# A network of two blocks with routed experts: the last expert's overflow block in one branch, and a hint for the branch on further blocks

## The chip, the cores and the metric

One core of one Trainium2 chip. The metric is the device time of one execution, in microseconds; the kernel before takes 1542.91 us (median of 3 runs, 1542.90 to 1544.29).

## What is computed

The input is 256 tokens of width 1024, all in float32. The first block has two layers. Each is a mixer (gated linear attention in layer 0, a gated linear recurrent unit, LRU, in layer 1), followed by a mixture of experts; shift, scale and gate of each come from a vector `c` through `ada_w`. The second block (weights `w_in`, `w_mod` and others) has three mixers side by side and a convolutional feed-forward part. What the change touches is the mixture of experts:

```python
scores = sigmoid(t @ router_w)
sel = scores + router_bias                     # 16 experts in 4 groups
grp = argmax over groups of the sum of the 2 largest sel in the group
expert_idx = the 2 largest sel inside grp      # 2 experts for each token
w = scores at expert_idx, divided by their sum
for e in range(16):
    he = silu(t @ w_gate[e]) * (t @ w_up[e])   # 1024 -> 512
    out = out + combine[:, e:e + 1] * (he @ w_down[e])   # 512 -> 1024
```

An expert's `combine` is zero for tokens that aren't routed to it, so only the routed tokens have to be worked on.

## The kernel before, in words

**An expert's tokens.** A rank says where a token stands among an expert's tokens. The first 64 tokens of an expert go through its main path: they are gathered by matmuls with one-hot matrices (`gather`, four experts at a time), go through `gate_up` (L904; SiLU and product L907 and L908), are transposed (`transp`, L913 and L915), go through `down` (L943; ACT L951 and DVE L954 scale the result into `y`), and `scatter` (L960) adds them with a one-hot matrix to `acc`, which stays in PSUM for a whole layer. `slots_of` (transposes L921, comparisons L923 and L924) makes the one-hot matrices `sa` for the scatter and `osa` for an overflow block.

**Overflow.** Where an expert has more than 64 tokens, the others go through blocks of 32. `vals[e]` is the number of such blocks, loaded into registers. A block has three parts: `block_x` (gather L988, weights L992, transposes L1001, scale and shift L1004 and L1005), `block_up` (L1013, transpose L1019, copy L1020) and `block_down` (L1027, scaling L1029 and L1030, scatter L1034). `blocks(e)` is an inner branch (L1045) with a loop in it, for the second block and more. With these inputs, experts 6 and 15 overflow in layer 0 and expert 12 in layer 1, each by one block, so the inner branch never enters its body.

**Where the branches stand.** Experts 0, 1 and 15 are *split*: a branch `up` behind gate and up (L1079) holds the inner branch, `block_x` and `block_up`, and a branch `ex` (L1100) at the expert's end holds `block_down`. The other experts have one branch, `ex`, with the whole block and then the inner branch. All five engines run each branch. `tc.mark_branch_hint_location` puts an instruction on each of the five engines that announces a branch, by its label, ahead of time, as one that is likely to jump (here: past the body). The outer branches have such a hint, ahead of the gate and up of their expert; the inner one has none.

**Weights.** `Stream` hands out weights from SBUF buffers of up to 2 MB, in one fixed order for the whole kernel: SP issues a transfer (L177 for gate and up, L179 for the others) as soon as a buffer is freed in the program and its readers are done. An expert holds three buffers: two halves of gate and up (read by L904 and L1013), and one of down (read by L943 and L1027). A split expert frees two of them behind its `up` branch and the third behind `ex`; the others free all three behind `ex`. Behind the last expert of layer 0 come the weights of the LRU layer (`ada_w`, first read by L442, and `lru_w_in`), behind that of layer 1 those of the second block: `w_in`, which ACT (L630) and DVE (L632) cut into pieces for the matmuls L641 to L643. The constants of the second block (`par_pk` among them) are loaded by L288, also on SP.

**The order of work** inside a stretch without branches is set by a list scheduler when the program is built; it moves half of the next expert's gate and up ahead of an expert's `ex` branch. The scatter of expert e is placed behind the gate and up of expert e + 1; the last expert's stands behind its `ex` branch, and behind that DVE adds `acc` to the state (L1112).

Of the kernel before, what the change touches and what calls it, by code (L numbers as in the profile page):

```python
# [20 lines left out]
NE = 16  # L21
# [212 lines left out]
class Net:  # L234
# [64 lines left out]
    def jobs(self):  # L299
# [32 lines left out]
        for n, j in self.late[0]:  # L332
            mod(n, j)
        self.marks["moe0"] = len(J)
        moe(0)
        self.marks["lru"] = len(J)
        w = A["lru_w_in"][0]
# [517 lines left out]
    def moe(self, l, m, late, aside={}):  # L855
        nc, tc = self.nc, self.tc
        shift, gate = m[:, 24:32], m[:, 40:48]
        with ExitStack() as st:
# [14 lines left out]
            vals = [nc.values_load(nblk[0:1, e:e + 1], min_val=0, max_val=6,  # L873
                                   skip_runtime_bounds_check_because="at most 256 tokens") for e in range(NE)]
# [98 lines left out]
            def tokens_of(oo, rk):  # L973

                for tt in range(2):
                    nc.vector.tensor_scalar(oo[:, tt], self.c("slots")[:, None, 0:32].to_broadcast([P, 4, 32]),
                                            rk[:, tt:tt + 1], None, op0=OP.is_equal)

            def block_x(e, oo):


                o = lambda tt: oo[:, tt].rearrange("p a b -> p (a b)")
                pg = [ps.tile([P, 512], F32, name="ps") for _ in range(2)]
                n = 0
                for tt in range(2):
                    for h in (hh, hl):
                        for c in range(2):
                            nc.tensor.matmul(pg[c], o(tt), h[:, tt, 512 * c:512 * c + 512], start=(n == 0), stop=(n == 3))  # L988
                        n += 1
                pw = ps.tile([P, 512], F32, name="ps")  # L990
                for tt in range(2):
                    nc.tensor.matmul(pw[:, :2], o(tt), whl[:, tt, e, :], start=(tt == 0), stop=(tt == 1))  # L992
                for g in range(4):
                    src = pg[g // 2][q(g), 256 * (g % 2):256 * (g % 2) + 256]
                    if g % 2:
                        nc.vector.tensor_copy(xt[q(g)], src)
                    else:
                        nc.scalar.activation(xt[q(g)], src, AF.Copy)
                pt = ps.tile([P, 512], F32, name="ps")
                for b in range(2):  # L1000
                    nc.tensor.transpose(pt[:, b * P:b * P + P], xt[:, b * P:b * P + P], self.ident)  # L1001
                quarters = lambda a: a.rearrange("p (b g s) -> p b g s", b=2, g=4)
                per_ft = lambda a: a.rearrange("p (g b) -> p b g", g=4)[:, :, :, None].to_broadcast([P, 2, 4, 32])
                nc.vector.tensor_tensor(quarters(xg), quarters(pt[:, :256]), per_ft(gs), op=OP.mult)  # L1004
                nc.vector.tensor_tensor(quarters(xg), quarters(xg), per_ft(shift), op=OP.add)  # L1005
                nc.vector.tensor_reduce(ow, pw[:, :2], axis=AX.X, op=OP.add)
# [35 lines left out]

            def blocks(e):

                with tc.If(vals[e] > 1):  # L1045
                    nc.vector.tensor_copy(rk, rank64[:, e, :])
                    nc.vector.tensor_copy(sc, sc64)
                    with tc.For_i(1, vals[e], 1):
                        nc.vector.tensor_scalar(rk, rk, 32.0, None, op0=OP.subtract)
                        nc.vector.tensor_scalar(sc, sc, 32.0, None, op0=OP.add)  # L1050
                        tokens_of(oo1, rk)
                        pt = ps.tile([P, 512], F32, name="ps")
                        for tt in range(2):
                            nc.tensor.transpose(pt[:, tt * P:tt * P + P], rank[:, tt, e:e + 1].to_broadcast([P, P]),
                                                self.ident)
                        nc.vector.tensor_scalar(osa1, pt[:, :T], sc, None, op0=OP.is_equal)
                        block_x(e, oo1)
                        block_up(e)
                        block_down(e, osa1)
# [8 lines left out]
            for e in range(NE):  # L1068
                g, j = e // 4, e % 4
                more = aside.get(e)  # L1070
                if more:
                    more(ps, sb)
                W[e] = [self.ws.take("moe") for _ in range(3)]
                split, end = e in (0, 1, NE - 1), e == NE - 1
                tc.mark_branch_hint_location(f"up{l}_{e}" if split else f"ex{l}_{e}", "LikelyTaken", engines=[mybir.EngineType.PE, mybir.EngineType.SP, mybir.EngineType.DVE, mybir.EngineType.Activation, mybir.EngineType.Pool])
                tokens_of(oo, rank64[:, e, :])
                he, last = gate_up(lambda k: XG[g][:, k, j, :], W[e])
                if split:
                    with tc.If(vals[e] > 0, label=f"up{l}_{e}"):  # L1079
                        blocks(e)  # L1080
                        block_x(e, oo)
                        block_up(e, "pgu")
                    self.ws.free(3 if more else 2)
                pt = ps.tile([P, 512], F32, name="ps")
                if split:
                    tc.mark_branch_hint_location(f"ex{l}_{e}", "LikelyTaken", engines=[mybir.EngineType.PE, mybir.EngineType.SP, mybir.EngineType.DVE, mybir.EngineType.Activation, mybir.EngineType.Pool])
                heT = transp(he, pt)
                if e:
                    with tc.issue_after(last):
                        scatter(*Y.pop(e - 1))  # L1090
                y = down(heT, W[e][2], WS[g][:, j:j + 1])
                with tc.issue_after(last):
                    Y[e] = y, slots_of(e, pt)
                    if g + 1 < 4 and j == 0:
                        onehot(g + 1)
                    if g + 1 < 4 and j == 3:
                        for i in range(4):
                            gather(g + 1, i)
                        slot_w(g + 1)
                with tc.If(vals[e] > 0, label=f"ex{l}_{e}"):  # L1100
                    if not split:
                        block_x(e, oo)
                        block_up(e)
                    block_down(e, osa, "pgu" if split else "py")
                    if not split:
                        blocks(e)
                if end:
                    scatter(*Y.pop(e))
                del W[e]
                self.ws.free(1 if split else 4 if more else 3)  # L1110
# [1072 lines left out]
```

## Time and profile before

| | |
|---|---|
| median of 3 runs | 1542.91 us |
| the profiled execution | 1545.11 us, its span 1543.3 us |
| TensorE's granted clock over the span | 0.975 of full speed |
| PE busy (matmuls) | 1436.0 us, 93% of the span |
| DVE, ACT, POOL busy | 808.2, 659.9, 76.0 us |
| DMA over the span | 406.25 MB, 263 GB/s on average |
| layer 0: mixer, then experts | to about 207 us, to 500 us |
| layer 1: mixer (LRU), then experts | to 645 us, to 921 us |
| second block | 921 us to the end |

How to read it: the span is the time from the first to the last instruction in the profile, and the profiled execution's own time is 1.8 us longer. An engine's busy time counts matmuls, vector and scalar work; branches and DMA issues belong to an engine's sequencer, shown with a q (PEq, SPq). In a timeline each row has a start, a duration and the work, and in brackets how long the engine stood idle before it and what ended that ("issue" where nothing the profile shows was waited for). Neighbouring instructions of one group are merged into one row.

### The profile page before, as it was taken

The numbers are of one execution on the slowest core, as the hardware profiler recorded it, in microseconds if no ns is written. First come the engines' busy times: TensorE is split into PE (matmuls) and PEld (weight loads), VectorE is DVE, ScalarE is ACT, GpSimd is POOL, SyncE is SP. The second block draws the span as 40 slices with busy tenths as digits, with TensorE's granted clock in tenths as the row PEclk, the third lists the DMA queues.
The fourth block names the chain that finished last, engine by engine and source line by source line (L and its number), as shares of the span: only waits on it lengthen the run. The fifth ranks groups of instructions, "written<-read, shape, count | busy, mean of one in ns | idle before, by whom it ended". The sixth has DMA issues, their size and how long they took to land. (4 is left out here: it accounts for less than half of the span.)

```text
span 1543.3 us, 24106 instructions
## 1 busy us (share of the span) xinstructions
PE 1436.0 (93%) x9234; PEld 995.1 (64%) x9234; DVE 808.2 (52%) x1930; ACT 659.9 (43%) x1347; POOL 76.0 (5%) x80
## 2 busy tenths in 40 slices
PE   5999978989897979889998889999999999999998
PEld 2565833434333658634434338898887889899998
DVE  3444531222222785422223237968876887876775
ACT  4534441212211565512123126666664565565553
POOL 0000110000000052200010000000000101100000
PEclk9999989999997999999999999999999999999999
DMA  9998586989999786786999864636634724995400
GB/s 362 386 386 297 207 336 255 342 316 360 393 392 379 280 315 239 297 325 237 395 394 391 306 222 141 218 114 215 220 137 136 254 74 165 318 362 195 137 1 28
DMA packets 193145, 406.25 MB, mean 263 GB/s; under 512 B 4514, under 2 KB 30754, under 8 KB 192691
## 3 DMA queue, kind: packets, MB, share of 16 engines
q1 hardware_dynamic: 192192, 402.75, 72.2%
q8 instruction: 121, 1.98, 0.5%
q10 hardware_dynamic: 754, 0.88, 0.2%
q14 instruction: 78, 0.63, 0.1%
HBM read 402.57 MB, written 1.05 MB: 262 GB/s over the span
## 5 line engine op out<-in xcount | busy, mean ns | idle before, releaser
L632 DVE TENSOR_TENSOR piece<-wt,piece 128x512 fp32r<-128x512 f32 (+1 forms) x364 | 276.2, 763 | 160.5 <-ACT piece L630 159.4
L630 ACT ACTIVATE piece<-wt 128x512 fp32r<-128x512 f32 (+1 forms) x368 | 248.4, 680 | 209.1 <-PE pd L643 154.3
L904 PE MATMUL pgu<-wt,xg 128*64 128x512 f32 x1024 | 252.5, 616 | 11.4 <-PEq L1100 6.2
L642 PE MATMUL pd<-hT,piece 128*128 128x256 f32 x624 | 177.6, 285 | 0.0
L641 PE MATMUL pd<-hT,piece 128*128 128x256 f32 x624 | 177.5, 285 | 0.0
L643 PE MATMUL pd<-hT,piece 128*128 128x256 f32 x624 | 176.8, 285 | 0.0
L904 PEld LDWEIGHTS pgu<-wt,xg 128*64 128x64 f32 x1024 | 74.8, 140 | 136.0 <-issue 130.0
L943 PE MATMUL py<-wt,heT 128*64 128x512 f32 x512 | 128.4, 616 | 3.8 <-ACT heT L915 3.8
L641 PEld LDWEIGHTS pd<-hT,piece 128*128 128x128 f32 x624 | 118.5, 190 | 4.8 <-ACT piece L630 2.2
L923 DVE TENSOR_SCALAR sa<-ps,par_cst 128x256 fp32r<-128x256 f32 x32 | 15.5, 484 | 201.6 <-issue 137.4
L642 PEld LDWEIGHTS pd<-hT,piece 128*128 128x128 f32 x624 | 118.6, 190 | 2.2 <-issue 2.0
L643 PEld LDWEIGHTS pd<-hT,piece 128*128 128x128 f32 x624 | 118.3, 190 | 2.1 <-issue 2.0
L951 ACT ACTIVATE y<-py,wsl 64x512 fp32r<-64x512 f32 x64 | 43.7, 683 | 174.0 <-PE py L943 157.7
L442 PE MATMUL pd<-wt,cond 128*32 128x512 f32 x576 | 86.5, 610 | 0.7 <-DMA wt<-ada_w 0.7
L943 PEld LDWEIGHTS py<-wt,heT 128*64 128x64 f32 x512 | 38.7, 141 | 70.7 <-issue 63.9
L907 ACT ACTIVATE he<-pgu 128x256 f32<-128x256 f32 x32 | 12.3, 384 | 145.2 <-PE pgu L904 135.9
L641 PE MATMUL pd<-s,piece 128*128 128x256 f32 x224 | 64.5, 289 | 3.5 <-ACT s L1274 2.3
L642 PE MATMUL pd<-piece,hT 128*128 128x512 f32 x160 | 66.1, 414 | 0.4 <-DVE piece L632 0.4
L643 PE MATMUL pd<-s,piece 128*128 128x256 f32 x224 | 63.4, 285 | 2.3 <-DVE piece L632 2.3
L643 PE MATMUL pd<-piece,hT 128*128 128x512 f32 x160 | 63.2, 398 | 0.0
L642 PE MATMUL pd<-s,piece 128*128 128x256 f32 x224 | 63.1, 283 | 0.0
L641 PE MATMUL pd<-piece,hT 128*128 128x512 f32 x160 | 57.9, 411 | 3.6 <-ACT piece L630 3.6
(595 smaller groups left out, 2879.0 us busy)
## 6 DMA issues: line engine op xcount, KB each, us to landing
wt<-moe_w_gate SPq DMA_DIRECT2D x64, 1024.0 KB, 11.2
wt<-moe_w_up SPq DMA_DIRECT2D x64, 1024.0 KB, 13.5
wt<-moe_w_down SPq DMA_DIRECT2D x32, 2048.0 KB, 15.6
wt<-ada_w SPq DMA_DIRECT2D x24, 2048.0 KB, 19.7
wt<-w_in SPq DMA_DIRECT2D x21, 2048.0 KB, 8.8
wt<-w_mod SPq DMA_DIRECT2D x12, 2048.0 KB, 8.5
wt<-w_up SPq DMA_DIRECT2D x22, 1024.0 KB, 12.3
wt<-gla_w_in SPq DMA_DIRECT2D x6, 2048.0 KB, 19.7
```

The lines of the kernel that those rows point to most:

```text
L442: nc.tensor.matmul(acc[32 * c:32 * c + 32, :], self.cond[:, k, :], w[:, k, :], start=(k2 == 0), stop=(k2 == 1))
L630: self.cast = nc.scalar.activation(hi, v, AF.Copy).ins
L632: (nc.gpsimd if low_on_pool else nc.vector).tensor_tensor(lo, v, hi.bitcast(F32), op=OP.subtract)
L641: mm(out, l[0], r[0], start=start, stop=False, **k)
L642: mm(out, l[0], r[1], start=False, stop=False, **k)
L643: mm(out, l[1], r[0], start=False, stop=stop, **k)
L904: last = nc.tensor.matmul(pgu[64 * hf:64 * hf + 64], xg(k), w[k // 4][:, :, k % 4, 256 * hf:256 * hf + 256], start=(k == 0), stop=(k == KT ...
L907: nc.scalar.activation(he, pgu[:, 0, :], AF.Silu)
L923: nc.vector.tensor_scalar(sa, pt[:, :T], self.c("slotcol"), None, op0=OP.is_equal)
L943: nc.tensor.matmul(py[64 * c:64 * c + 64, :], heT[:, b, 64 * hf:64 * hf + 64], wd[:, 2 * hf + b, 512 * c:512 * c + 512], start=(n == 0), s ...
L951: nc.scalar.activation(y[0:64, c], py[h], AF.Copy, scale=wsl[h])
```

## The change

Expert 15 is no longer split, in both layers. The inner branch gets a label, and those experts that aren't split run a hint for it where their `ex` branch has been entered, so only where the expert overflows.

```diff
--- before.py
+++ after.py
@@ -1042,7 +1042,7 @@
 
             def blocks(e):
 
-                with tc.If(vals[e] > 1):
+                with tc.If(vals[e] > 1, label=f"in{l}_{e}"):
                     nc.vector.tensor_copy(rk, rank64[:, e, :])
                     nc.vector.tensor_copy(sc, sc64)
                     with tc.For_i(1, vals[e], 1):
@@ -1071,7 +1071,7 @@
                 if more:
                     more(ps, sb)
                 W[e] = [self.ws.take("moe") for _ in range(3)]
-                split, end = e in (0, 1, NE - 1), e == NE - 1
+                split, end = e in (0, 1), e == NE - 1
                 tc.mark_branch_hint_location(f"up{l}_{e}" if split else f"ex{l}_{e}", "LikelyTaken", engines=[mybir.EngineType.PE, mybir.EngineType.SP, mybir.EngineType.DVE, mybir.EngineType.Activation, mybir.EngineType.Pool])
                 tokens_of(oo, rank64[:, e, :])
                 he, last = gate_up(lambda k: XG[g][:, k, j, :], W[e])
@@ -1099,6 +1099,7 @@
                         slot_w(g + 1)
                 with tc.If(vals[e] > 0, label=f"ex{l}_{e}"):
                     if not split:
+                        tc.mark_branch_hint_location(f"in{l}_{e}", "LikelyTaken", engines=[mybir.EngineType.PE, mybir.EngineType.SP, mybir.EngineType.DVE, mybir.EngineType.Activation, mybir.EngineType.Pool])
                         block_x(e, oo)
                         block_up(e)
                     block_down(e, osa, "pgu" if split else "py")
```

## Rows read from the trace of the kernel before

**Rows 1.** Windows: stretch, length, busy PE, PEld, DVE, ACT, POOL, PEclk, DMA share, GB/s.

```profile
207.00:500.00 293.00, 262.22 (x1381) 115.25 (x1382) 68.46 (x160) 57.34 (x114) 1.52 (x1) 0.94 0.92 345
921.00:1543.00 622.00, 612.69 (x4556) 556.48 (x4555) 476.73 (x1119) 364.41 (x776) 23.79 (x21) 1.00 0.51 172
```

**Rows 2.** Costliest groups of the page (busy us, mean ns, idle before).

```profile
L904 PE MATMUL pgu<-wt,xg 128*64 128x512 f32 x1024 | 252.5, 616 | 11.4 <-PEq L1100 6.2
...
L442 PE MATMUL pd<-wt,cond 128*32 128x512 f32 x576 | 86.5, 610 | 0.7 <-DMA wt<-ada_w 0.7
```

**Rows 3.** Timeline of PE, layer 0, expert 15 (start, us, work, [idle <-releaser]).

```profile
464.09 3.65 PE L904 MATMUL pgu<-wt,xg 128*64 128x512 f32 x16 [0.40 <-PEq L1100]
473.24 1.01 PE L988 MATMUL ps<-hh,oo 128*128 128x512 f32 x2 [5.49 <-issue]
...
493.45 0.39 PE L1034 MATMUL acc<-osa,ot 32*128 32x256 f32 x4 [0.64 <-ACT ot L1029]
...
494.84 2.05 PE L960 MATMUL acc<-sa,y 128*128 128x256 f32 x8 [0.25 <-DVE y L954]
```

**Rows 4.** Line L1045, the inner branch: who waited for it (us, times).

```profile
  PE ps L988: 5.5, 1
```

**Rows 5.** Timeline of PE, layer 1, expert 12, whose overflow block is entered.

```profile
858.03 0.43 PE L921 MATMUL ps<-par_pk,rank 128*128 128x128 f32 x2
...
861.98 0.73 PE L988 MATMUL ps<-hh,oo 128*128 128x512 f32 x2
...
876.97 0.29 PE L1034 MATMUL acc<-osa,og 32*128 32x256 f32 x4
877.90 4.49 PE L904 MATMUL pgu<-wt,xg 128*64 128x512 f32 x12 [0.65 <-PEq L1045]
```

**Rows 6.** Timeline of PE, layer 0, expert 14.

```profile
450.60 3.65 PE L904 MATMUL pgu<-wt,xg 128*64 128x512 f32 x16 [0.40 <-PEq L1100]
...
456.09 3.65 PE L943 MATMUL py<-wt,heT 128*64 128x512 f32 x16 [0.47 <-ACT heT L915]
459.68 0.43 PE L921 MATMUL ps<-par_pk,rank 128*128 128x128 f32 x2
```

**Rows 7.** Timeline of DVE, layer 1, expert 12.

```profile
858.97 0.47 DVE L924 TENSOR_SCALAR osa<-ps,par_cst 128x256 fp32r<-128x256 f32 x1
```

**Rows 8.** Timeline of PE, layer 0, behind expert 6's overflow block.

```profile
346.09 1.21 PE L960 MATMUL acc<-sa,y 128*128 128x256 f32 x8 [0.55 <-DVE oo L976]
```

**Rows 9.** Timeline of PE, layer 1, expert 15 and what follows it.

```profile
906.29 3.65 PE L904 MATMUL pgu<-wt,xg 128*64 128x512 f32 x16 [0.40 <-PEq L1100]
910.56 0.38 PE L960 MATMUL acc<-sa,y 128*128 128x256 f32 x1 [0.61 <-PEq L1079]
...
912.34 3.65 PE L943 MATMUL py<-wt,heT 128*64 128x512 f32 x16
915.92 0.43 PE L921 MATMUL ps<-par_pk,rank 128*128 128x128 f32 x2
919.06 2.08 PE L960 MATMUL acc<-sa,y 128*128 128x256 f32 x8 [2.71 <-DVE y L954]
921.91 0.58 PE L641 MATMUL pd<-wt,piece 128*128 128x256 f32 x1 [0.77 <-ACT piece L630]
```

**Rows 10.** Timeline of SP: the first issues of w_in.

```profile
910.40 6.45 SPq L179 DMA_DIRECT2D wt<-w_in  x3
```

**Rows 11.** DMA issues: the first w_in, and the first two (last: us to landing).

```profile
wt<-w_in SPq DMA_DIRECT2D x1, 2048.0 KB, 8.8
...
wt<-w_in SPq DMA_DIRECT2D x2, 2048.0 KB, 11.3
```

**Rows 12.** Timeline of ACT at the start of the second block.

```profile
921.23 2.19 ACT L630 ACTIVATE piece<-wt 128x512 fp32r<-128x512 f32 x4 [3.76 <-PE acc L960]
```

**Rows 13.** Timeline of DVE in the second block's start.

```profile
931.27 0.41 DVE L1367 TENSOR_SCALAR par_pk<-par_pk 128x24 f32<-128x24 f32 x4
```

**Rows 14.** Timeline of PE, layer 0: the longest idle time at an ex branch.

```profile
404.22 5.02 PE L904 MATMUL pgu<-wt,xg 128*64 128x512 f32 x16 [3.48 <-PEq L1100]
```
## How it was expected to go

> **What bounds the kernel.** I read the stretches first, then the groups of instructions, then the timelines around the last expert. In the stretch of the first layer's experts the PE is busy 262.22 of 293.00 us, and after 921 us, in the second block, 612.69 of 622.00 [rows 1]: TensorE bounds both, and a delay that reaches the second block has hardly anything to hide in. Weights are not late in the expert stages: the 1024 matmuls of L904 waited 11.4 us in all, most often for PE's sequencer at the ex branch L1100, and the 576 of L442, the first to read weights after the first layer's experts, waited 0.7 us for theirs [rows 2]. So in these stages it counts when PE stands still at a branch, and in what order the ends of a layer are done.
>
> **Layer 0: the last expert has an overflow block.** Before, its order on PE is gate and up (L904), the up branch with the block's first half, the main down projection, the ex branch with the block's second half, the scatter. From the end of L904 (464.09 + 3.65 = 467.74) to the end of the last scatter (494.84 + 2.05 = 496.89) it takes 29.15 us [rows 3]. 5.49 us of it is PE idle ahead of the block's first matmul, L988 [rows 3], and the view of line L1045 gives it to the inner branch (nblk > 1) that the up branch opens with [rows 4]. That branch jumps, since no expert here has two blocks, and nothing has announced its target. After the idle the first pair of L988 takes 1.01 us, where expert 12's takes 0.73 [rows 3, 5].
>
> After the change expert 15 goes as the others do, and each piece has a row:
> - From the end of L904 to the end of the slot transposes L921: expert 14 goes from 450.60 + 3.65 = 454.25 to 459.68 + 0.43 = 460.11, 5.86 us [rows 6].
> - Between L921 and the block: expert 12 of layer 1 has an overflow block in the new order. There half of the next expert's L904 stands between, and the block follows without idle time [rows 5]; the last expert has no next one. The block's second PSUM tile needs L924, which ends at 859.44, 0.98 us after L921 (858.46) [rows 5, 7]; the branch alone costs 0.40 [rows 6]. The first matmul of a pair needs only the first tile, so I take 0.8, bounds 0.4 and 1.0.
> - The whole block: 861.98 to 877.26, 15.28 us [rows 5]. Matmuls as slow as those behind the 5.49 would add 1.1 (four pairs of L988 at 1.01 less 0.73); the 0.8 is a short idle, and I take none.
> - The inner branch, now at the block's end: expert 12 shows 0.65 us idle behind it, expert 6 of layer 0, 0.55 [rows 5, 8]. I take 0.55, for here too the scatter follows. Above stands the 5.49 of [rows 3]; with the hint, below stands 0.
> - The last scatter: 1.21 as for expert 6 [rows 8]; before it took 2.05 [rows 3].
>
> Sum: 5.86 + 0.8 + 15.28 + 0.55 + 1.21 = 23.7, a gain of 29.15 - 23.7 = **5.45 us**. The small terms at their ends (0.4 or 1.0 for 0.8, slow pairs, 0 for 0.55) give 4.1 to 6.4. The weights of the next stage leave it be: its first reader, L442, never waited more than 0.7 [rows 2]. SP issues one transfer for it behind the block's first half; that half ends at about the same time in either order, the 5.49 of idle time giving place to the 5.86 of the main down projection.
>
> **Layer 1: the last expert has no overflow.** Here the up branch costs little: from the end of L904 (909.94) to L943 (912.34) 2.40 us [rows 9], for expert 14 456.09 - 454.25 = 1.84 [rows 6], so 0.56 goes. But the up branch was also the place behind which two of the expert's three weight buffers came free. SP issues w_in, the first weights of the second block, at 910.40, the second right behind, and the third behind the ex branch, 6.45 us for all [rows 10]. The first lands 8.8 us after its issue, at 919.2 [rows 11], and the first ACT piece made of it starts at 921.23, having waited for the last scatter [rows 12]; L641 follows at 921.91 [rows 9]. So now the transfer is hidden with 2 us to spare.
>
> After the change all three buffers are freed behind the ex branch. PE leaves L921 at 916.35 less 0.56, so the issue is at about 915.9 and the landing at 915.9 + 8.8 = 924.7: **3.5 us later** than the piece starts now. The cover is gone: what hid this transfer was the down projection L943, behind which it is now issued. An issue that waits for L943 alone would be 0.4 earlier, which gives 3.0 as lower end. The 0.56, and whatever the scatter gains (it waits 2.71 us for y now, which in the new order stands ahead of the branch [rows 9]), go into waiting for w_in and count nothing.
>
> Queued behind on SP are three constants of the second block. The first w_in lands after 8.8 us and the first two after 11.3 on average, so the second after 13.8, some 5 to 5.5 behind the first [rows 11]; three in a row end at 934.7 to 935.7, the constants behind that, say 936. DVE reads par_pk at 931.27 [rows 13], shifted 934.8, so they come up to 1.4 late. PE has other matmuls then: 0 to 1.4, I take 0.5. Layer 1 pays **4.0 us**, bounds 3.0 and 4.9.
>
> **The hints.** One more instruction on five engines, run only where a block is entered: three times. The profile shows no price for it. Below, it saves the idle time behind the inner branch at experts 6 and 12, 0.55 + 0.65 = 1.2 [rows 5, 8]; above, the code lies one instruction further per expert, and a branch that now gets its code in time may not: the longest such idle time in this layer is 3.48 [rows 14]. I take -0.2, since most branches show about 0.4 and that bound is one place.
>
> Sum: -5.45 + 4.0 - 0.2 = **-1.65 us**. The profiled execution took 1545.11 us with a span of 1543.3, and 1.8 around it; the median of the runs is 1542.91. A difference of stages applies to either: 1543.5 for the profiled one, **1541.3** for the median. About 0.2%, 3.1 us, is what a measurement of this kernel can tell from no change.
>
> **Rivals.**
> *The w_in transfer costs nothing.* Then layer 1 keeps its 0.56 and about 1 us of the scatter's wait, and the sum is -5.45 - 1.5 - 0.2 = -7.1: 1535.8. For it speaks that SP waits per buffer and not per branch, if gate and up are known to be read at 909.94. Against it: the third w_in, whose buffer is read by L943 and freed behind the ex branch, goes out only at about 916.5 [rows 10], and PE has under 10 us of idle time in the whole second block [rows 1].
> *The stall moves with the branch (slower).* The inner branch still jumps, now from the end of the body. If its target's code isn't there, PE stands 5.49 instead of 0.55 ahead of the last scatter: layer 0 gains 0.5 and layer 1 pays 4.0, sum +3.3: 1546.2. It decides at the last scatter of layer 0: over 4 us idle there and the whole is slower. Against it speak the 0.55 and 0.65 of [rows 5, 8], where that branch had no hint and stood in this very place; for it, that the last expert is followed by other code, and the hint, 15 us ahead, may fetch what is then not needed.
> [...]
> *The hint shifts other stalls.* One place like that of [rows 14] more or less is 3.5 either way: 1544.8 or 1537.8. No row says which.
> *The change doesn't do what it says*: the hint is run but too late to help, in a stretch where the DMA is busy for 0.92 of the time with weights [rows 1]. Then -0.2 becomes 0 and the time is 1541.5; it can't be told from the forecast by the time.
>
> **How the numbers follow.** The forecast gets 0.58, with a range of its own from 1538.5 to 1543.5; the free transfer 0.14; the moved stall 0.14; shifted stalls 0.14, half each way. Faster by over 0.2% is below 1539.8: the free transfer, the fast half of the shifts (0.07) and 0.10 of the forecast, where layer 0 gains 6.4 or layer 1 pays 3.0; together 0.31. Slower is above 1546.0: 0.11 of the moved stall (the rest with early constants), and 0.03 of the slow shifts, with constants at their late end; together 0.14. What is left, 0.55, is within 0.2%. The range of 1536.5 to 1546.0 leaves out most of the moved stall and the fuller half of the free transfer, about 0.2.
>
> **What would show it.** Right: in layer 0 no idle time over 1.2 us between expert 15's L904 and L988, a first pair of L988 at 0.73, L960 behind at most 1 us idle, 23 to 25 us from L904's end to the scatter's; in layer 1 three w_in issued at about 916, and the first piece L630 waiting for DMA instead of the scatter, 3 to 4 us later after L904's end than now (11.3 us). Wrong: w_in still issued at the end of L904, or its landing ahead of the scatter (first rival); over 4 us idle ahead of layer 0's last scatter (second); new idle times of 2 us or more at branches of other experts (third).

## The result, and the profile after

The changed kernel takes 1554.8 us (median of 4 runs, 1553.03 to 1557.19), the kernel before 1542.91 beside it: a ratio of 1.0071, 95% interval 1.0058 to 1.0084. It is slower by 11 to 12 us where a gain of 1.65 was forecast, and outside the range of 1536.5 to 1546.0. The profiled execution took 1554.96 us, its span 1552.8 (before 1545.11 and 1543.3). Three slow executions (1654.21, 4665.88 and 4866.0 us) are counted in the medians of the first experiments, which without them are 1548.26 for the branch alone, 1541.19 for layer 0 only and 1543.08 for the kernel before, and left out of the ratios, none of which is exactly the quotient of two medians.

The most direct way to find out where is to take instructions that both kernels have, and see how far apart they are in the two profiles. PE's timeline after, at the places that matter (start, duration, work, idle time before; "..." stands for rows left out):

```profile
406.49 3.65 PE L904 MATMUL pgu<-wt,xg 128*64 128x512 f32 x16 [3.46 <-PEq L1100]
...
428.88 4.44 PE L904 MATMUL pgu<-wt,xg 128*64 128x512 f32 x12 [3.67 <-PEq L1100]
...
470.03 3.65 PE L904 MATMUL pgu<-wt,xg 128*64 128x512 f32 x16 [0.40 <-PEq L1100]
...
475.53 0.43 PE L921 MATMUL ps<-par_pk,rank 128*128 128x128 f32 x2 [0.47 <-ACT heT L915]
475.89 3.65 PE L943 MATMUL py<-wt,heT 128*64 128x512 f32 x16
479.47 0.73 PE L988 MATMUL ps<-hh,oo 128*128 128x512 f32 x2
...
484.96 3.66 PE L1013 MATMUL py<-wt,oxg 128*32 128x256 f32 x64 [0.98 <-DVE oxg L1005]
...
493.52 0.29 PE L1034 MATMUL acc<-osa,og 32*128 32x256 f32 x4
497.30 2.07 PE L960 MATMUL acc<-sa,y 128*128 128x256 f32 x8 [3.48 <-PEq L1045]
...
676.08 9.72 PE L904 MATMUL pgu<-wt,xg 128*64 128x512 f32 x32 [5.79 <-DVEq L1100]
...
910.13 3.65 PE L904 MATMUL pgu<-wt,xg 128*64 128x512 f32 x16 [0.40 <-PEq L1100]
...
915.99 3.65 PE L943 MATMUL py<-wt,heT 128*64 128x512 f32 x16
...
929.86 0.58 PE L641 MATMUL pd<-wt,piece 128*128 128x256 f32 x1 [6.32 <-ACT piece L630]
```

Two rows of PE's timeline before that weren't needed ahead of the prediction: the matching ones for 428.88 and 676.08.

```profile
424.60 2.79 PE L904 MATMUL pgu<-wt,xg 128*64 128x512 f32 x12 [0.29 <-PEq L1100]
...
669.76 7.09 PE L904 MATMUL pgu<-wt,xg 128*64 128x512 f32 x32 [1.15 <-DVEq L1100]
```

| place | before | after | apart | change in that stretch |
|---|---|---|---|---|
| L904 behind the ex branch with the longest wait [rows 14] | 404.22 | 406.49 | +2.27 | +2.27 (1.3 of it by 207 us, in the mixer) |
| second half of expert 15's L904, layer 0 [rows 3] | 464.09 | 470.03 | +5.94 | +3.67 |
| end of the last scatter of layer 0 [rows 3] | 496.89 | 499.37 | +2.48 | -3.46 |
| expert 1's L904, layer 1 | 669.76 | 676.08 | +6.32 | +3.84 |
| second half of expert 15's L904, layer 1 [rows 9] | 906.29 | 910.13 | +3.84 | -2.48 |
| first L641 of the second block [rows 9] | 921.91 | 929.86 | +7.95 | +4.11 |
| end of the span | 1543.3 | 1552.8 | +9.5 | +1.55 |

What the reader is to see: the place that the change is about, expert 15 of layer 0, has gained 3.46 us. The end of layer 1 and what follows from it lose 4.11 + 1.55 = 5.66. And there are losses where nothing was edited but one instruction: PE stands still ahead of expert 12's L904 in layer 0 for 3.67 us where it stood 0.29, and ahead of expert 1's in layer 1 for 5.79 where it stood 1.15. After both the matmuls are slow for a while (12 of L904 take 4.44 instead of 2.79, and 32 take 9.72 instead of 7.09), so each costs about 1.7 to 2.6 us more than its idle time. They are slow where TensorE's granted clock is 0.50: in 428.8 to 432.2 and in 674.6 to 681.4, with 1.00 around both. Not every such wait is followed by it. Behind the 3.46 at 406.49 the clock stays at 1.00 and the 16 of L904 take 3.65, where before they took 5.02 behind 3.48 [rows 14] with a mean clock of 0.72; this gives back 1.4. Two windows after (columns as in [rows 1]):

```profile
406.49:410.14 3.65, 3.65 (x17) 1.30 (x17) 0.23 (x2) 0.00 (x0) 0.00 (x0) 1.00 1.03 407
428.88:432.20 3.32, 3.32 (x8) 1.03 (x10) 0.33 (x2) 0.00 (x0) 0.00 (x0) 0.50 1.04 382
```

The wait at 676.08 is ended by DVE's sequencer at the ex branch L1100: there it was DVE that hung, idle for 4.87 us ahead of its L954, and PE waited for it. Some of it comes back soon (expert 1's up branch in layer 1, which waited 2.45 us before, waits 0.37), and by expert 15 of layer 1 2.48 of the 3.84 are back. Without the last expert of layer 0 (-3.46) and the end of layer 1 with what follows (+5.66), 9.5 + 3.46 - 5.66 = 7.3 us of loss are left, 1.3 of them in layer 0's mixer, ahead of all edits.

**What the idle time at 428.88 is.** The view of line L1100 gives the duration of the compare-and-branch on PE's sequencer (after, then before):

```profile
L1100 PEldq COMPARE_BRANCH  x1: 6016/6016/6016, 422.6 to 422.6; - x1
```

```profile
L1100 PEldq COMPARE_BRANCH  x1: 331/331/331, 421.7 to 421.7; - x1
```

The branch itself takes 6.02 us instead of 0.33. While it hangs, one transfer of instructions of 0.02 MB starts on queue q8, between 426.0 and 426.2 (the DMA view of that stretch after; packets, MB, share of 16 engines):

```profile
q1 hardware_dynamic: 29, 0.08, 107.4%
q8 instruction: 1, 0.02, 34.3%
```

On q8 there is none between 422.6 and 426.0 (another queue, q14, has one of 0.01 MB), with the weights' queue q1 at a share of 102.0%. The branch ends at 428.6. This is no single case: in the profiles before and after, 30 of 87 compare-and-branches on PE's sequencer take over 1.5 us, and at each of the 30 one transfer of this size on q8 ends 1.3 to 1.6 us before the branch does; at none of the other 57 does one end while it lasts. So where PE hangs at a branch, such a transfer of instructions ends just before it goes on. That it is the branch's code, and that the weights hold it up, is likely, but not shown apart.

**The end of layer 1.** ACT's and SP's timelines after, the landing of the first w_in (last column), and DVE's read of the constants:

```profile
929.18 2.19 ACT L630 ACTIVATE piece<-wt 128x512 fp32r<-128x512 f32 x4 [1.33 <-DMA wt<-w_in]
...
919.77 6.19 SPq L179 DMA_DIRECT2D wt<-w_in  x3
...
wt<-w_in SPq DMA_DIRECT2D x1, 2048.0 KB, 9.3
...
940.68 0.40 DVE L1368 TENSOR_SCALAR par_pk<-par_pk 128x24 f32<-128x24 f32 x4
```

All three w_in are issued as the down projection ends (915.99 + 3.65 = 919.64), and the first piece waits for DMA, where it waited for the scatter [rows 12]. L1368 (L1367 before) stands 940.68 - 931.27 = 9.41 us later [rows 13], 1.46 more than the first L641: the constants are late as well.

### The profile page after: what moved, and what is told of

It reads as the page before. It is cut to its first block, busy times and chain, and to the rows that moved or that the text cites. A ratio compares the mean times of both kernels' runs of the same rounds, so it can differ in the third digit from the quotient of the medians.

```text
span 1552.8 us, 24102 instructions
## 1 busy us (share of the span) xinstructions
PE 1434.6 (92%) x9234; PEld 992.2 (64%) x9234; DVE 810.2 (52%) x1930; ACT 660.6 (43%) x1347; POOL 76.8 (5%) x80
## 5 line engine op out<-in xcount | busy, mean ns | idle before, releaser
L904 PE MATMUL pgu<-wt,xg 128*64 128x512 f32 x1024 | 253.3, 617 | 19.4 <-PEq L1100 9.5
L641 PE MATMUL pd<-hT,piece 128*128 128x256 f32 x624 | 177.6, 285 | 0.0
L904 PEld LDWEIGHTS pgu<-wt,xg 128*64 128x64 f32 x1024 | 74.1, 140 | 145.7 <-issue 139.7
L943 PE MATMUL py<-wt,heT 128*64 128x512 f32 x512 | 127.3, 611 | 3.8 <-ACT heT L915 3.8
L641 PEld LDWEIGHTS pd<-hT,piece 128*128 128x128 f32 x624 | 118.5, 190 | 4.7 <-ACT piece L630 2.2
L943 PEld LDWEIGHTS py<-wt,heT 128*64 128x64 f32 x512 | 38.5, 139 | 69.7 <-issue 62.9
L641 PE MATMUL pd<-s,piece 128*128 128x256 f32 x224 | 64.3, 289 | 3.5 <-ACT s L1275 2.3
L642 PE MATMUL pd<-piece,hT 128*128 128x512 f32 x160 | 66.2, 415 | 0.2 <-DVE piece L632 0.2
L954 DVE SCALAR_TENSOR_TENSOR y<-py,wsl,y 64x512 fp32r<-64x512 f32 x64 | 48.0, 750 | 35.1 <-ACTq L1100 17.8
L643 PE MATMUL pd<-piece,hT 128*128 128x512 f32 x160 | 63.2, 398 | 0.0
```

The source lines that it names most:

```text
L641: mm(out, l[0], r[0], start=start, stop=False, **k)
L642: mm(out, l[0], r[1], start=False, stop=False, **k)
L643: mm(out, l[1], r[0], start=False, stop=stop, **k)
L904: last = nc.tensor.matmul(pgu[64 * hf:64 * hf + 64], xg(k), w[k // 4][:, :, k % 4, 256 * hf:256 * hf + 256], start=(k == 0), stop=(k == KT ...
L943: nc.tensor.matmul(py[64 * c:64 * c + 64, :], heT[:, b, 64 * hf:64 * hf + 64], wd[:, 2 * hf + b, 512 * c:512 * c + 512], start=(n == 0), s ...
L954: nc.vector.scalar_tensor_tensor(y[64:128, c], py[h], wsl[h], y[0:64, c].bitcast(F32), op0=OP.mult, op1=OP.subtract)
```

## The experiments

A run's median is put beside that of the kernel before on the same chip. Theory A says that most of the loss is code position: the hint, an instruction per expert and engine, moves the code behind it, and a branch waits or doesn't wait for its code depending on where it stands. Its rivals are B (the branch change does it all) and D (the hints do it when they run). C holds that the gain of layer 0 is lost again in layer 1's branches.

**The hint alone.** Expert 15 stays split.

```diff
-                with tc.If(vals[e] > 1):
+                with tc.If(vals[e] > 1, label=f"in{l}_{e}"):
...
                     if not split:
+                        tc.mark_branch_hint_location(f"in{l}_{e}", "LikelyTaken", ...)
                         block_x(e, oo)
```

> Expert 15 stays split; only the inner branch's label and its hint are added. Theory A (code position): the hint instruction, one per expert and engine, moves all later code, and with it the places where an engine waits for its instructions; so PE's idle time of 3.67 us ahead of expert 12's L904 in layer 0 (0.29 before) is here too, with the 1.7 us of slow matmuls behind it, and the time is 1546 to 1552 us, depending on what the shift does in layer 1. Theory B (the branch change does it all): no new idle time ahead of expert 12, 1541 to 1545 us.

1553.01 us against 1543.57, ratio 1.0052 (1.0036 to 1.0069). PE's timeline at two places that waited 0.29 before, experts 12 of layer 0 and one of layer 1:

```profile
428.29 4.78 PE L904 MATMUL pgu<-wt,xg 128*64 128x512 f32 x12 [3.89 <-PEq L1100]
...
794.38 2.07 PE L960 MATMUL acc<-sa,y 128*128 128x256 f32 x8 [3.39 <-PEq L1100]
```

Before, these rows stand at 424.60 (0.29) and 786.73 (0.29 as well). The hint by itself costs 8 to 10 us, a little over the range of theory A: theory B falls.

**The same instruction where it never runs.** It stands in the body of the inner branch, which no expert enters here.

```diff
+                with tc.If(vals[e] > 1, label=f"in{l}_{e}"):
+                    if e not in (0, 1, NE - 1):
+                        tc.mark_branch_hint_location(f"in{l}_{e}", "LikelyTaken", ...)
```

> Expert 15 stays split; the hint instruction of the other experts stands in the body of the inner branch, which never runs with these inputs: the later code is moved as in the run with the hint alone, and nothing more is executed. Theory A: the same new idle time of about 3.7 us ahead of expert 12's L904 in layer 0 and the same total as the run with the hint alone, within 2 us. Theory D (the hint, when it runs, fetches the wrong code): as before, 1541 to 1545 us.

1554.76 us, ratio 1.0067 (1.0050 to 1.0083), and the idle times are at the same two places:

```profile
427.78 5.39 PE L904 MATMUL pgu<-wt,xg 128*64 128x512 f32 x12 [2.55 <-PEq L1102]
...
794.89 1.83 PE L960 MATMUL acc<-sa,y 128*128 128x256 f32 x8 [3.33 <-PEq L1102]
```

An instruction that isn't run costs as much as one that is: theory D falls, and what is left is where the code stands. The first wait is shorter than expected (2.55 us, not 3.7). The label of the inner branch isn't the cause: the last two experiments below have it on every inner branch and are faster than the kernel before.

**One branch for expert 15, without label and hint.**

```diff
-                split, end = e in (0, 1, NE - 1), e == NE - 1
+                split, end = e in (0, 1), e == NE - 1
```

> Expert 15 has one branch, and there is no label and no hint. Theory A: no new idle time at expert 12 of layer 0, since the code up to expert 15 stands where it stood; expert 15 of layer 0 takes 24 to 26 us from the end of L904 to the end of the scatter instead of 29.15; the end of layer 1 pays 5 to 6 us for w_in; so 1543 to 1548 us, more or less by what the shorter code moves in layer 1. Theory B: 1552 to 1556 us. If the hint had shortened the inner branch of expert 15, the idle time ahead of the last scatter of layer 0 is over 3.48 us here.

1549.32 us, ratio 1.0032 (1.0016 to 1.0047), just above theory A's range and short of theory B's. The same kernel again, for its profile:

> The kernel with one branch for expert 15 in both layers and no hint, once more, for its profile: in layer 0 23 to 26 us from the end of expert 15's L904 to the end of the scatter; first L641 of the second block 7 to 9 us after the end of L943; idle time ahead of expert 12's L904 under 0.5 us. If the hint made the inner branch at expert 15's end shorter, the idle time ahead of the last scatter of layer 0 is over 4 us here, where it is 3.48 with the hint; if it doesn't matter, 3.2 to 3.6.

1546.18 us against 1543.4, ratio 1.0015 (1.0005 to 1.0025). PE's timeline of that run:

```profile
423.94 2.79 PE L904 MATMUL pgu<-wt,xg 128*64 128x512 f32 x12 [0.29 <-PEq L1100]
...
463.43 3.65 PE L904 MATMUL pgu<-wt,xg 128*64 128x512 f32 x16 [0.40 <-PEq L1100]
...
490.42 2.07 PE L960 MATMUL acc<-sa,y 128*128 128x256 f32 x8 [3.20 <-PEq L1045]
...
905.86 3.65 PE L943 MATMUL py<-wt,heT 128*64 128x512 f32 x16
...
918.62 0.58 PE L641 MATMUL pd<-wt,piece 128*128 128x256 f32 x1 [5.00 <-ACT piece L630]
```

This time it lies in theory A's range. Expert 12's L904 (423.94) waits 0.29 us at its branch, as before. Layer 0's last expert takes 490.42 + 2.07 - (463.43 + 3.65) = 25.41 us, as with the hint (25.69). The inner branch costs 3.20 without its hint and 3.48 with it: the hint did nothing for the branch it announces. In the other two blocks too it left things as they were: 0.55 at expert 6 and 0.67 at expert 12 after, 0.55 and 0.65 before [rows 5, 8]. L641 comes 918.62 - 909.51 = 9.1 us after the end of L943, just over the 7 to 9 expected.

**The two layers apart.**

```diff
-                split, end = e in (0, 1, NE - 1), e == NE - 1
+                split, end = e in (0, 1) or (l and e == NE - 1), e == NE - 1        # layer 0 only
...
+                split, end = e in (0, 1) or (not l and e == NE - 1), e == NE - 1    # layer 1 only
```

> Expert 15 has one branch in layer 0 and stays split in layer 1; no hint. Both theories agree that w_in is issued at the end of layer 1's last L904 and its first piece waits for the scatter. Theory A: layer 0 gains 3.5 to 5.5 us, 1537 to 1541 us, unless the shorter code moves a wait in layer 1. Theory C (the gain of layer 0 is lost again before layer 1 ends, in its branches): 1542 to 1545 us, with longer idle times at the first experts of layer 1.

> Expert 15 has one branch in layer 1 and stays split in layer 0; no hint, so all code up to the end of layer 1 stands where it stood. Theory A (w_in is issued 5.5 us later, after the down projection, and its first piece waits for it): first L641 6 to 8 us after where it is in the kernel before, some more for the constants, so 1548 to 1551 us. If the end of layer 1 costs only the 4.0 that was predicted: 1546 to 1547.5 us. If the loss in the run without hints came from moved code: 1541 to 1545 us.

Layer 0 only: 1541.6 us against 1543.57, ratio 0.9992 (0.9978 to 1.0005), a small gain that isn't clear of no change, and between the ranges of theories A and C. Layer 1 only: 1549.47 against 1544.0, ratio 1.0029 (1.0019 to 1.0039). In the first the inner branch is the rest of the wait; in the second all code up to the end of layer 1 stands where it stood, and w_in is the loss:

```profile
491.17 2.07 PE L960 MATMUL acc<-sa,y 128*128 128x256 f32 x8 [3.30 <-PEq L1045]
```

```profile
905.18 3.65 PE L904 MATMUL pgu<-wt,xg 128*64 128x512 f32 x16 [0.40 <-PEq L1100]
...
924.95 0.58 PE L641 MATMUL pd<-wt,piece 128*128 128x256 f32 x1 [6.36 <-ACT piece L630]
```

From L904 to L641 it is 19.77 us, before 921.91 - 906.29 = 15.62: 4.15 more, as in the changed kernel (4.11), and not the 6 to 8 that were expected. The spans differ by 1547.7 - 1543.3 = 4.4 although this run stood 1.1 ahead at L904, so the end of layer 1 and what follows it cost 5.5 in all, and theory A's range of 1548 to 1551 holds for the total. Theory C isn't needed for the totals: by the medians of 1548.26, 1541.19 and 1543.08 named at the result, -1.9 for layer 0 and +5.5 for layer 1 add up to 3.6, within the 2.8 to 5.2 of the runs with both. But the sign that it named is in the profile of layer 0 only: PE waits 2.36 us ahead of expert 1's L913 in layer 1 (at 677.62), where it did not wait before, and the lead over the kernel before falls from 4.4 us to 1.4 there; by expert 15 it is 5.0 again.

**Ten instructions, and 256.** The kernel before, with instructions that never run in the inner branch's body of one expert.

```diff
+                with tc.If(vals[e] > 1, label=f"in{l}_{e}"):
+                    for _ in range(10 if (l, e) == (0, 2) else 0):      # 256 in the other run
+                        tc.mark_branch_hint_location(f"in{l}_{e}", "LikelyTaken", ...)
```

> The kernel before with ten instructions per engine that never run, in the inner branch's body of expert 2 of layer 0: all later code stands ten instructions further, as far as it does ahead of expert 12 in the changed kernel. Theory A (what counts is where the code stands): the idle time of 2.5 to 3.9 us ahead of expert 12's L904 in layer 0 is here, and the time is 1545 to 1555 us. Theory D (it takes the hints at each expert): no such idle time, 1541 to 1545 us.

> As the run with ten, but with 256 instructions. Theory A with code fetched in blocks of 256 instructions: every later place stands where it stood in its block, so idle times are those of the kernel before, 3.5 us ahead of L904 at about 404, none over 1 us ahead of expert 12's L904, and the time is 1541 to 1545 us. If any longer code costs, or the blocks have another size, it is like the run with ten or worse, 1545 to 1556 us.

With ten: 1543.0 us (1533.68 to 1544.47; four of ten runs under 1540) against 1544.0, ratio 0.9981 (0.9965 to 0.9997). With 256: 1550.21, ratio 1.0033 (1.0019 to 1.0047). Both predictions of theory A missed the time, and the one for ten instructions the place of the waits as well. PE's timelines, first with ten (the execution of 1533.77 us, one of the four under 1540; what the other six waited for is not on record), then with 256, then L608 before:

```profile
398.57 3.65 PE L904 MATMUL pgu<-wt,xg 128*64 128x512 f32 x16 [0.40 <-PEq L1102]
...
417.55 2.79 PE L904 MATMUL pgu<-wt,xg 128*64 128x512 f32 x12 [0.29 <-PEq L1102]
...
464.29 1.19 PE L988 MATMUL ps<-hh,oo 128*128 128x512 f32 x2 [3.60 <-PEq L1045]
...
781.00 2.07 PE L960 MATMUL acc<-sa,y 128*128 128x256 f32 x8 [3.47 <-PEq L1102]
...
807.06 0.58 PE L608 MATMUL ps<-ones,wt 128*128 128x1 f32 x4 [0.50 <-DVE oo L976]
```

```profile
275.39 0.66 PE L913 MATMUL ps<-par_pk,he 128*128 128x128 f32 x2 [4.71 <-DVEq L1102]
...
409.49 5.03 PE L904 MATMUL pgu<-wt,xg 128*64 128x512 f32 x16 [3.48 <-PEq L1102]
...
478.52 1.01 PE L988 MATMUL ps<-hh,oo 128*128 128x512 f32 x2 [5.50 <-issue]
...
818.40 0.91 PE L608 MATMUL ps<-ones,wt 128*128 128x1 f32 x4 [3.74 <-DVE oo L976]
```

```profile
813.23 0.98 PE L608 MATMUL ps<-ones,wt 128*128 128x1 f32 x4 [3.80 <-DVE oo L976]
```

With ten, expert 12 (417.55) does not wait, against the expectation; but the 3.48 of [rows 14] has gone to 0.40, the 5.49 of [rows 3] to 3.60, the 3.80 that L608 had waited in layer 1 to 0.50, and a new 3.47 stands at 781. With 256, every idle time behind the added code is that of the kernel before to within 0.1 (3.48, 5.50, 3.74), while shorter shifts change some of them: places 256 instructions apart gave the same waits. The loss (5.3 us in the profile) is at one new place, 4.71 us at 275.39, right behind the code that was made longer. By an estimate from the trace of the kernel before, 256 instructions of PE are about one transfer on q8: from 921 to 1543 us q8 has 36 of them, 0.59 MB together, while PE runs 4556 matmuls and 4555 weight loads [rows 1], 253 to a transfer. The estimate takes all of q8 for PE's code, which is not shown; nor is it shown where in PE's code a transfer begins.

**Hints one expert earlier, on PE.** On top of the branch in layer 0 only:

```diff
+                others = [mybir.EngineType.SP, mybir.EngineType.DVE, ...]      # all but PE
+                label = f"up{l}_{e}" if split else f"ex{l}_{e}"
+                tc.mark_branch_hint_location(label, "LikelyTaken", engines=others if e > 1 else others + [mybir.EngineType.PE])
+                if e and not end:
+                    nxt = l and e + 1 == NE - 1
+                    tc.mark_branch_hint_location(f"up{l}_{e + 1}" if nxt else f"ex{l}_{e + 1}", "LikelyTaken", engines=[mybir.EngineType.PE])
```

> As the run with one branch in layer 0 only (1541.6 us), but on PE the hint for an expert's branch is run one expert earlier (from expert 2 on). If PE's idle times behind the branches come from code that is fetched too late under full DMA queues, and PE keeps a target for that long, those ahead of L904 at about 402 (3.44) and of L608 at about 811 (3.56) go, and the time is 1532 to 1539 us. If only one target is kept, or it is dropped by then, idle times of 3 us and more come at most experts: over 1560 us.

1571.89 us, ratio 1.0181 (1.0164 to 1.0198). The view of PE's waits, here and in the run with layer 0 only (waited for; us, times, longest):

```profile
PE acc L960 <- PEq L1105: 16.5, 15, 3.3
...
PE pgu L904 <- PEq L1105: 11.5, 8, 3.7
```

```profile
PE pgu L904 <- PEq L1100: 6.1, 8, 3.4
...
PE acc L960 <- PEq L1100: 4.4, 15, 0.4
```

Behind the ex branches PE waits 28.0 us instead of 10.5. The time is in the range of the second case expected: with the earlier hints the kernel takes some 30 us more than without (1541.6). But the waits of 3 us and more are not at most experts, as a single kept target would have it. The edit also makes PE's code one instruction longer from expert 1 on, so the place of the code is not held fixed here.

**Layer 0 only, with the code moved by 10, 40 and 120.** The same instructions that never run, in expert 2 of layer 0.

> One branch for expert 15 in layer 0 only (1541.6 us) and the ten instructions that never run. If the gain of 3.5 us in layer 0 and the idle times that the ten instructions took away (3.48 ahead of L904 at 404, 3.80 ahead of L608) are independent, this is the fastest: 1532 to 1540 us. If the places interact (the code behind expert 15 is shorter by 8 than in the run with ten alone), layer 1 has other idle times: 1538 to 1546 us.

> The same with 40 instructions. The place of every branch in its block of 256 is new, so no run before says which stall. Theory A: the total lies anywhere from 1532 to 1552 us and all of the difference to the run without shift is in idle time at branches of 1.4 us and more; the 3.3 us ahead of the last scatter of layer 0 may change, since the end of expert 15 now lies across the border of a block. If only the edit's own work counts: 1541 to 1543 us.

> The same with 120 instructions. Theory A: again 1532 to 1552 us, with other places of idle time than with 40. If only the edit's own work counts: 1541 to 1543 us.

1545.12, 1549.47 and 1547.19 us; ratios 1.0002 (0.9988 to 1.0016), 1.0039 (1.0026 to 1.0052) and 1.0022 (1.0012 to 1.0033). Without moved code it was 1541.6: the same work goes from 1541.6 to 1549.5 when code that never runs moves the rest. The gain of ten instructions does not add to that of layer 0. With 40, the second half of theory A's expectation missed: of the 13.0 us between the profiled spans (1551.4, and 1538.4 without moved code) 11.8 are PE longer busy with the same 9234 matmuls (1441.1 and 1429.3 us) and only 1.2 idle time. The mean granted clock is 0.972 there and 0.979 here, so most of this difference is matmuls that took longer, at a lower mean clock, and not the waits themselves. With 120 the wait ahead of the last scatter of layer 0 is gone, and a new one of 5.09 stands behind the longer code, at 275. PE's timeline with 120:

```profile
470.28 3.65 PE L904 MATMUL pgu<-wt,xg 128*64 128x512 f32 x16 [0.40 <-PEq L1102]
...
496.30 1.21 PE L960 MATMUL acc<-sa,y 128*128 128x256 f32 x8 [0.54 <-PEq L1045]
```

From the end of L904 to that of the scatter: 496.30 + 1.21 - 473.93 = 23.58 us, where 23.7 was predicted.

**Moving only PE's code, only ahead of expert 15.** This asks whether the place of expert 15's end alone decides its inner branch. One run moves it by 120 and puts 142 more ahead of layer 1, so that from there on PE's code stands 256 further than before (120 + 142, less the 6 counted by which expert 15 got shorter; the expectation of the run with ten has 8, and no profile shows either); the other leaves the 142 out.

```diff
+                with tc.If(vals[e] > 1, label=f"in{l}_{e}"):
+                    for _ in range({(0, 14): 120, (1, 0): 142}.get((l, e), 0)):
+                        tc.mark_branch_hint_location(f"in{l}_{e}", "LikelyTaken", engines=[PE])
```

> One branch for expert 15 in layer 0 only, no hint; on PE alone, 120 instructions that never run move expert 15's end in layer 0 to the place that it has in the run with 120, and 142 more ahead of layer 1 move all later PE code to 256 instructions behind where it stands in the kernel before. Theory A (PE's place in its blocks decides): idle time ahead of the last scatter of layer 0 0.5 to 0.7 us, 23 to 24.5 us from the end of expert 15's L904 to the end of the scatter, idle times in layer 1 as before (3.7 to 3.8 ahead of L608), total 1536 to 1540 us, faster than both kernels. If it was the run's own timing and not the place: 3.2 to 3.5 us idle there, 1540 to 1544 us. If 120 instructions to jump over cost by themselves: a new idle time of 4 to 5 us behind expert 14, 1544 us or more.

> The same without the 142, so that layer 1's PE code stands 114 instructions further than before, as it does in the run with 120. Theory A: layer 0 as in the run with the 142, and layer 1 with its own idle times, so up to 5 us either way: 1534 to 1545 us.

1537.12 us against 1545.13, ratio 0.9957 (0.9943 to 0.9970), and 1537.37, ratio 0.9961 (0.9946 to 0.9976): faster than both kernels, by 6 to 8 us than the one before. PE's timeline with both insertions:

```profile
463.96 3.65 PE L904 MATMUL pgu<-wt,xg 128*64 128x512 f32 x16 [0.40 <-PEq L1102]
...
488.29 1.20 PE L960 MATMUL acc<-sa,y 128*128 128x256 f32 x8 [0.54 <-PEq L1045]
...
807.38 0.58 PE L608 MATMUL ps<-ones,wt 128*128 128x1 f32 x4 [3.55 <-DVE oo L976]
```

Without the 142, the row of the last scatter is:

```profile
488.92 1.21 PE L960 MATMUL acc<-sa,y 128*128 128x256 f32 x8 [0.55 <-PEq L1045]
```

From the end of L904 to the end of the scatter it is 488.29 + 1.20 - 467.61 = 21.88 us, 7.27 less than before. So the wait behind expert 15's inner branch is settled: it is set by where PE's code stands, and goes with 120 instructions that do nothing. Layer 1 shows that not every place matters: its waits are those of the kernel before (3.55 ahead of L608, 3.80 there) but for 2.08 ahead of expert 1's L913, and the run without the 142, where PE's code stands 142 instructions less far on, has the same ones (3.68 and 2.59).

## Why the prediction was wrong

**Reading of the kernel before.** Right: what is late at the end of layer 1 goes through, and idle time of PE around a branch sets expert 15's time. Wrong: the 5.49 us was put down to the inner branch and its target. The view of L1045 and the timeline of PE's weight loads before, around expert 15 of layer 0:

```profile
L1045 PEldq COMPARE_BRANCH  x1: 2619/2619/2619, 464.7 to 464.7; - x1
```

```profile
469.04 0.19 PEld L988 LDWEIGHTS ps<-hh,oo 128*128 128x128 f32 x1 [2.18 <-ACTq L1045]
473.24 0.29 PEld L988 LDWEIGHTS ps<-hh,oo 128*128 128x128 f32 x1 [4.01 <-issue]
```

The branch ended at 467.3, before L904 did (467.74), and the first weights of L988 were loaded at 469.04; most of the idle time, 4.01 us, lies behind that load, while an instruction transfer runs on q8 (470.8 to 471.9, so it ends 1.3 us before PE goes on, as at the long branches). So most of the 5.49 lies behind the branch, with that transfer in it, and is not the branch itself; that it was code which came late is likely. The runs with the hint alone, with the hint not run and with ten instructions moved it: 3.54 to 3.60 us idle, and there it is the branch that hangs (6.2 to 6.3 us).

**Layer 0: 5.45 us predicted, 3.46 measured**, within neither the sum nor the bounds of 4.1 to 6.4. The steps one by one: from L904's end (473.68) to L988 5.79 us, where 5.86 + 0.8 stood, because L921 now runs ahead of L943 and L924 is done in time; the block 479.47 to 493.81 = 14.34 instead of 15.28, with the 64 matmuls of L1013 in 3.66 us instead of 5.35 (granted clock 1.00 there, 0.50 at expert 12 before, in 867.8 to 871.2); the inner branch 3.48 instead of 0.55; the scatter 2.07 instead of 1.21 (clock 0.50 from 497.1 on). The step that failed is "The inner branch, now at the block's end: ... I take 0.55, for here too the scatter follows": the rows of experts 6 and 12 have the branch in the same order, but at another place of the code. Where the place is changed, by 120 instructions, it is 0.54 to 0.55. That the sum is then 23.58 with 120 instructions, where 23.7 was predicted, is partly luck: L1013 ran at a clock of 0.50 for a part there, as at expert 12 (5.35 us), and with PE's code alone moved the sum is 21.88.

**Layer 1: 4.0 us predicted (3.0 to 4.9), 5.66 measured**, 5.5 in the run with layer 1 only. The mechanism was right up to the first L641: the issue 919.77 - 913.78 = 5.99 us after the end of L904 (predicted 915.9 - 909.94 = 5.96), the piece waiting for DMA, the constants late behind it. Two sizes were off: the transfer took 9.3 us instead of 8.8, so L641 lost 4.1 instead of 3.5, and behind it 1.55 were lost where 0.5 was taken for the constants, of 0 to 1.4. Of these, 1.15 are there by 1000 us; that all of it hangs on the late constants is likely and not shown. Another 0.9 comes at about 1350 us, where the granted clock is 0.50 from 1353.8 to 1357.2 and was 1.00 before, behind the same 2.19 us of idle time ahead of L530; the profiles with the hint not run and with ten instructions, whose layer 1 ends as before, have such a stretch too, so it isn't due to the branch change. The last instructions give 0.5 back.

**The hints: -0.2 us predicted, 8 to 10 measured alone (1553.01 against 1543.57, ratio 1.0052), and 6.5 to 8.6 on top of the branch change (1554.8 against 1548.26 and 1546.18).** This is the step that made the prediction wrong: "One more instruction on five engines, run only where a block is entered", and the -0.2 that was taken because "that bound is one place". The instruction was costed by when it runs, and is paid for where it stands. The rival "the hint shifts other stalls" named the mechanism, but took one place and its idle time alone, 3.5 us, either way. There were two such places of 3.7 and 5.8 us in the changed kernel, and the matmuls at a clock of 0.50 behind them (1.7 and 2.6); a part came back, and 7.3 us is what the profile shows net, the mixer's 1.3 included. The clock of 0.50 behind a wait is in no term of the sum: for L988 alone the prediction weighs 1.1 us of it, and takes none.

**The rivals.** The free transfer was wrong, since w_in was issued behind the down projection. The moved stall came half true: 3.48 us, short of the 4 from which it was to decide, and due to the place of the code and not to other code behind the last expert. "The change doesn't do what it says" was right for the hint: with it 3.48, without 3.20. The sign of the third rival, new idle times of 2 us or more at branches of other experts, came, and the hints cost 8 to 10 us alone where it had 3.5.

**What stays open.** Why a branch waits at one place and not at another: expert 12's did with the hints at each expert and not with ten instructions in one expert, though its code stands equally far along in both (the profile with ten is of one of the four executions under 1540 us, and the others may differ). What was loaded earlier may count too, and no run here takes that apart. Nor is it shown why PE waited more with hints that come earlier (28.0 us and not 10.5), or why the clock falls to 0.50 behind one wait (3.67 us) and not behind another of about that length (3.46).

## What to carry to other kernels

In a stretch where the DMA queues are full of weights (share 0.92 [rows 1]), PE stood 3 to 6 us at a branch or 0.3, and which of them changed with where the code stands; an edit that adds instructions ahead of such branches moved the time here by some 10 us for reasons that aren't its own. So its worth is seen stage by stage, at the instructions that both kernels have, or with its code length varied. Before a buffer is freed later, ask which transfer it starts and what it hid behind: freeing two weight buffers 5.5 us later made the first matmul of the next stage 4.1 us late, at the one place where PE had nothing else to do. One branch in layer 0 alone, with PE's code placed so that PE waits only 0.54 us behind the last branch, took 1537.1 us.

## What the runs showed that was not expected

An instruction that is never run cost as much (1554.76 us) as the same one run (1553.01). Ten of them, in one place, made the kernel before faster in four of ten runs (1533.7 to 1538.4 against 1542.7 to 1544.5), so one and the same code also falls one way or the other by timing. In the profile of one of these four, 6.8 of the 11.3 us by which its span is shorter are the same matmuls in less time (PE busy 1429.2 instead of 1436.0 us). The 64 matmuls L1013 took 3.66 us in the block of expert 15 and 5.35 in those of experts 6 and 12, and in the run with 120 instructions 5.35 there too. The granted clock goes with it: 1.00 in the first (484.96 to 488.62), and 0.50 in 486.4 to 489.8 in the run with 120. Why the clock was granted differently in blocks of the same work is not shown.
